# A delta-rule recurrence's DRAM round trip on GpSimd's DMA queue, its merge begun ten steps later, and the latent scan's output products grouped by shape

## The chip, the cores and the metric

The kernel runs on one core of one Trainium2 chip, in one launch. The time is device microseconds (us) of an execution, and the median of several is compared. The engines are named as in the profile: PE is TensorE's matmul stream, PEld its weight loads, DVE VectorE, ACT ScalarE, POOL GpSimd, and SP SyncE, whose queue (SPq) issues nearly all DMAs.

## The reference

Two blocks in a row, all in float32, on 256 positions of 1024 channels. The first has two layers: a norm, an input projection, windowed attention and a pooling mixer, an output projection, and a feed-forward part with 4096 channels. The second has one layer and three branches (a gated delta rule, a short convolution, a Fourier mix), a gated merge and a SwiGLU. The change touches the delta rule alone, which runs in both directions, first over a context of 256 positions and from its end state over the latent positions:

```python
a = jnp.where(strict, jnp.einsum("bhnid,bhnjd->bhnij", kb, k) * decay, 0.0)
t_inv = lax.linalg.triangular_solve(a + eye, eye, left_side=True, lower=True, unit_diagonal=True)
...
def step(s, inp):
    u_i, w_i, qg_i, kd_i, attn_i, gl_i = inp
    v_new = u_i - jnp.einsum("bhcd,bhde->bhce", w_i, s)
    o_i = jnp.einsum("bhcd,bhde->bhce", qg_i, s) + jnp.einsum("bhij,bhje->bhie", attn_i, v_new)
    s = s * jnp.exp(gl_i)[..., None, None] + jnp.einsum("bhcd,bhce->bhde", kd_i, v_new)
    return s, o_i
```

There are 4 chunks of 64 positions, 4 heads of 128 channels and 2 directions, so 32 lower triangular matrices of 64 x 64 are inverted for the context and 32 for the latent positions. Only the latent scan gives outputs.

## The kernel before

**Weights.** Nearly all of PE's time goes into products with weights, which stream through the core once. A weight tile is 128 x 1024. SP loads it into `wst` (`weights`, L256; three buffers, 512 KB each); ACT rounds it to `wh` (L262); DVE subtracts to get the rest, `wl` (L263), each in two halves of 512. `mm3` then makes three products per piece (`wh` with the two halves of the activations, `wl` with the first), all issued at L272. A tile gives 24 matmuls of 256 columns. A load waits for a free `wst`, so for the `wl` of three tiles before; `wl` waits for `wh`, and `wh` for the load.

**Side work.** The second block's modulation and delta rule run beside these products as a generator. `tick` is called once per weight tile and advances it by a rate: 1.2 steps a tile for the context (beside the first block's last feed-forward part), 0.8 for the latent recurrence (beside the short convolution's and the gates' products, woven with the modulation's `w_mod` sums, `wmst`, on DVE). A `yield` ends a step; a scheduler then sets each engine's order, and `issue_after(i)` places an instruction behind `i` on its engine.

**The inverse.** `dn_base` inverts the 16 x 16 diagonal blocks of the triangles on POOL. POOL folds them from `dA` into `ac`; four DMAs write `ac` to DRAM (`there`, L1265, 64 partitions each, in pieces of 16 numbers), one reads them back with a block per partition (`bl`, L1269). Two copies make `blt` (ACT L1273 and DVE L1274, the second transposed). POOL then does fifteen rounds of a product `bo` (L1282) and a subtraction `bz` (L1283), and a transposed copy `bzt` (L1287). Four DMAs write the result to DRAM (`back`, L1291) and four fetch it in the old layout (`xc`, L1299, again in pieces of 16 numbers). The waits between are yields: three after each of the four DMA legs (`wait_dma`), and five among the rounds, 17 in all. `dn_merge` starts with eight multiplications on DVE (`Tm` and `U` from `xc`, L1314), and builds the 64 x 64 inverses from there with PE. There are two such trips, for the context and for the latent positions.

**The scan.** `dn_scan` takes four steps, in each of which both directions handle a chunk. For the eight pairs of head and direction of a latent step it issues two products into the same output tile: the state with the decayed query (`S,qg`; 128 rows of contraction, 64 columns of weights) and the new values with the attention (`dv,att`; 64 and 64), one pair after the other. A product of float32 stands in the trace as two matmul records.

Of the kernel before, what the change touches and what calls it, by code (L numbers as in the profile page):

```python
# [9 lines left out]
F32 = mybir.dt.float32  # L10
F32R = mybir.dt.float32r
I32 = mybir.dt.int32
AF = mybir.ActivationFunctionType
OP = mybir.AluOpType
AX = mybir.AxisListType

P = 128
# [213 lines left out]
class Net:  # L231
# [18 lines left out]
    def weights(self, src, cut=1):  # L250

        nc = self.nc
        st = self.wst.tile([P, 1024], F32, name="wst")
        for c in range(cut):
            cs = slice(c * 1024 // cut, (c + 1) * 1024 // cut)
            nc.sync.dma_start(st[:, cs], src[:, cs])  # L256
        wh = self.wsp.tile([P, 1024], F32R, name="wh")
        wl = self.wsp.tile([P, 1024], F32R, name="wl")
        n = 1024 // self.cutw
        for c in range(0, 1024, n):  # L260
            with self.behind():
                nc.scalar.activation(wh[:, c:c + n], st[:, c:c + n], AF.Copy)  # L262
            (nc.gpsimd if self.onpool > 0 else nc.vector).tensor_tensor(wl[:, c:c + n], st[:, c:c + n], wh[:, c:c + n].bitcast(F32), op=OP.subtract)  # L263
        self.onpool -= 1
        return wh, wl

# [381 lines left out]
    def drain(self):  # L648
        if self.side is not None:
            self.busy = True  # L650
            run(self.side)
            self.busy = False
        self.side = None
# [594 lines left out]
    def dn_base(self, A, X):  # L1248


        nc, pool = self.nc, self.nc.gpsimd
        m = self.k["d_blk"][:, None].to_broadcast([P, 4, 4, 16])
        ac = self.b2.tile([P, 2, 2, 4, 16], F32, name="ac", bufs=1)
        for t in range(2):
            for a in range(2):
                w = self.b2.tile([P, 4, 4, 16], F32, name="bw", tag="gm", bufs=2)
                pool.tensor_tensor(w, A[t][:, a].rearrange("p h (b j) -> p h b j", b=4), m, op=OP.mult)
                pool.tensor_tensor(w[:, :, 0:2], w[:, :, 0:2], w[:, :, 2:4], op=OP.add)
                pool.tensor_tensor(ac[:, a, t], w[:, :, 0], w[:, :, 1], op=OP.add)
            yield  # L1260
        there = self.dram.tile([2, 8, P, 16], F32, name="there")
        for hb in range(2):
            for a in range(2):
                s = slice(64 * hb, 64 * hb + 64)
                nc.sync.dma_start(there[a ^ hb].rearrange("n p j -> p n j")[s], ac[s, a].rearrange("p t h j -> p (t h) j"))  # L1265
        for _ in range(self.wait_dma):
            yield
        L = self.b2.tile([P, 16, 16], F32, name="bl", bufs=1)
        nc.sync.dma_start(L, there.rearrange("d n (q i) j -> (d n q) i j", i=16))  # L1269
        for _ in range(self.wait_dma):  # L1270
            yield
        lt = self.b2.tile([P, 16, 16], F32, name="blt", bufs=1)
        nc.scalar.activation(lt[0:64], L[0:64], AF.Copy)  # L1273
        nc.vector.tensor_copy(lt[64:P], L[64:P].rearrange("p i j -> p j i"))  # L1274
        Z = self.b2.tile([P, 16, 16], F32, name="bz", bufs=1)
        pool.memset(Z, 0.0)
        pool.memset(Z.rearrange("p i j -> p (i j)")[:, 0:256:17], 1.0)
        for j in range(15):
            n, c = 15 - j, j + 1
            o = self.b2.tile([P, 8, 16], F32, name="bo", bufs=1).rearrange("p i j -> p (i j)")[:, 0:n * c]  # L1280
            o = o.rearrange("p (i j) -> p i j", j=c)
            pool.tensor_tensor(o, lt[:, c:, j:c].to_broadcast([P, n, c]), Z[:, j:c, 0:c].to_broadcast([P, n, c]), op=OP.mult)  # L1282
            pool.tensor_tensor(Z[:, c:, 0:c], Z[:, c:, 0:c], o, op=OP.subtract)  # L1283
            if j % 3 == 2:
                yield
        zt = self.b2.tile([P, 16, 16], F32, name="bzt", bufs=1)
        (pool if self.ztp else nc.vector).tensor_copy(zt, Z.rearrange("p i j -> p j i"))  # L1287
        back = self.dram.tile([2, 2, 8, P, 16], F32, name="back")
        for dr in range(2):
            for x in range(2):  # L1290
                nc.sync.dma_start(back[dr, x].rearrange("n (q i) j -> (n q) (i j)", i=16),  # L1291
                               (Z, zt)[x ^ dr][64 * dr:64 * dr + 64].rearrange("p i j -> p (i j)"))
        for _ in range(self.wait_dma):
            yield
        xc = self.b2.tile([P, 2, 2, 2, 4, 16], F32, name="xc", bufs=1)
        for hb in range(2):
            for a in range(2):
                s = slice(64 * hb, 64 * hb + 64)
                nc.sync.dma_start(xc[s, a].rearrange("p x t h j -> p (x t h) j"),  # L1299
                               back[a ^ hb].rearrange("x n p j -> p (x n) j")[s])  # L1300
        for _ in range(self.wait_dma):
            yield
        X["X"] = xc

    def dn_merge(self, d, t, e, A, xc):

        nc, k = self.nc, self.k
        full = [P, 2, 4, CHUNK]
        Tm = self.b2.tile(full, F32, name="Tm")
        U = self.b2.tile(full, F32, name="U")  # L1310
        m = k["d_blk"][:, None].to_broadcast([P, 4, 4, 16])
        for x, o in enumerate((Tm, U)):
            for a in range(2):
                nc.vector.tensor_mul(o[:, a].rearrange("p h (b j) -> p h b j", b=4),  # L1314
                                     xc[:, a, x, t][:, :, None, :].to_broadcast([P, 4, 4, 16]), m)
        for n in range(2):
            al = self.b2.tile(full, F32, name="al")
            nc.vector.tensor_mul(al, A, k["d_lev"][:, :, n][:, :, None, :].to_broadcast(full))
            yb = self.bank().rearrange("p (a h j) -> p a h j", a=2, h=4)
            for a, h, hb, s in self.halves():  # L1320
                self.mm(yb[s, a, h], al[s, a, h], U[s, a, h])
            y = self.b2.tile(full, F32, name="dy")
            nc.scalar.activation(y.rearrange("p a h j -> p (a h j)"), yb.rearrange("p a h j -> p (a h j)"), AF.Copy)
            yield
            ub = self.bank().rearrange("p (a h j) -> p a h j", a=2, h=4)
            for a, h, hb, s in self.halves():
                self.mm(ub[s, a, h], Tm[s, a, h], y[s, a, h])
            if n == 0:
                yield
                tb = self.bank().rearrange("p (a h j) -> p a h j", a=2, h=4)  # L1330
                for a, h, hb, s in self.halves():
                    self.mm(tb[s, a, h], y[s, a, h], Tm[s, a, h])
            nc.vector.tensor_sub(U, U, ub)
            if n == 0:
                nc.vector.tensor_sub(Tm, Tm, tb)
            yield
        W = self.b2.tile(full, F32, name="W")
        nc.vector.tensor_mul(W, U, d["beta"][:, t][:, :, :, None].to_broadcast(full))
        e["W"] = W
# [8 lines left out]
    def dn_scan(self, d, e, S, res):  # L1348
        nc = self.nc
        lat = "q" in d  # L1350
        S = S[-1] if S else None
        if lat:
            ot = [self.dbank().rearrange("p j (q c) -> p (j q) c", c=P) for _ in range(2)]
            res.extend(ot)
        hh = [(h, hb, slice(64 * hb, 64 * hb + 64)) for h in range(4) for hb in range(2)]
        full = [P, 4, P]
        for step, (t, a) in enumerate(STEPS):
            x = e[t]
# [24 lines left out]
            if lat:  # L1383
                v1 = self.sm.tile(full, F32, name="dv1", tag="w2k", bufs=self.nw2k)
                nc.scalar.activation(v1.rearrange("p h c -> p (h c)"), nb.rearrange("p h c -> p (h c)"), AF.Copy)
                q = self.dn_query(d, t, a)
                for h, hb, s in hh:
                    o = ot[t][s, h]
                    self.mm(o, q[:, h, s], S[:, 4 * (a ^ hb) + h], step < 2 and h == 0, False, True)
                    self.mm(o, x["att"][s, a, h], v1[s, h], False, step >= 2, True)  # L1390
            yield
            if last:
                break
# [13 lines left out]
            S = N  # L1407
# [313 lines left out]
    def run(self):  # L1721
# [35 lines left out]
        self.ctx_rate = 1.2  # L1757
        self.scan_rate = 1.8
        self.mod_rate = 0.8
        self.wait_dma = 3  # L1760
        self.mod_parts = (((1, 0, 2), (3,), (4, 5)), ((1, 0, 2), (), (3, 4, 5)), ((1, 0, 2, 3), (), (4, 5)), ((1, 0), (), (2, 3, 4, 5)))[1]
        with ExitStack() as ctx:
            self.ctx = ctx
# [45 lines left out]
```

## Time and profile before

| | |
|---|---|
| median of 3 runs | 1269.43 us (1269.08 to 1270.76) |
| profiled execution | 1270.11 us, span 1268.3 us |
| mean granted clock of PE | 0.975 |
| PE busy | 1202.9 us, 95% of the span |
| DVE, ACT, POOL busy | 900.3, 636.4, 100.1 us |
| DMA | 221.44 MB, mean 175 GB/s |

A share of the whole span says little of one place: the windows split the busy time by stretches, the waits say which instruction an engine waited for, and the timelines give single instructions with the idle time before them and its releaser in brackets. In a row, `out<-in` names tiles, `128*64` is a matmul's rows of contraction and columns of weights, and `xN` is a count. The busy time of POOL is rough.

### The profile page before, as it was taken

How to read it: one execution, taken by the hardware profiler on the slowest of the kernel's cores; microseconds unless marked ns; L12 is line 12 of the kernel's file. 1: busy time of each engine (PE TensorE's matmuls, PEld its weight loads, DVE VectorE, ACT ScalarE, POOL GpSimd, SP SyncE). 2: the span in 40 equal slices, each digit the busy share in tenths (PEclk: the TensorE clock that was granted, in tenths of full speed). 3: DMA queues.
4: the chain of work that ended last, by engine and by line, in shares of the span. 5: the costliest groups of instructions: out<-in, count | busy, mean ns of one | idle time of the engine just before them, and what ended most of it. 6: DMA issues, size and time to landing. Idle time of an engine off the chain costs nothing.

```text
span 1268.3 us, 24741 instructions
## 1 busy us (share of the span) xinstructions
PE 1202.9 (95%) x9858; PEld 1130.2 (89%) x9858; DVE 900.3 (71%) x1786; ACT 636.4 (50%) x1249; POOL 100.1 (8%) x183
## 2 busy tenths in 40 slices
PE   8999999999999989979999799998999997999997
PEld 6779999999977989979999789898888796999997
DVE  6998986557986587636558899987555476555555
ACT  5655445455655555534545656444432354544444
POOL 1000000000100000330000410542000002000000
PEclk9999999999999989989999899998999997999998
DMA  6656787554543535346544415687432252655552
GB/s 231 237 193 217 253 298 255 188 187 149 186 163 127 200 128 186 105 140 202 184 163 139 158 67 188 229 275 234 148 111 74 76 189 85 196 180 190 184 183 83
DMA packets 78388, 221.44 MB, mean 175 GB/s; under 512 B 22336, under 2 KB 24512, under 8 KB 78272
## 3 DMA queue, kind: packets, MB, share of 16 engines
q1 hardware_dynamic: 78272, 219.86, 51.7%
q8 instruction: 77, 1.26, 0.4%
q14 instruction: 39, 0.32, 0.1%
HBM read 218.00 MB, written 1.84 MB: 173 GB/s over the span
## 4 chain that ended last, share of the span: by engine, by line
PE 62%; issue 14%; DVE 12%; DMA 5%; POOL 3%; ACT 2%; SPq 1%; DVEq 0%; ACTq 0%; POOLq 0%
PE acc L272 35%; PE bank L272 26%; DVE wl L263 3%; DMA wmst<-w_mod 2%; POOL bo L1282 1%; POOL bz L1283 1%; ACT wh L262 1%; DVE wmst L880 1%; DVE cy L1034 1%; PE bank L563 1%; DMA wst<-w_in 1%; DVE xl L296 1%; PE bank L368 1%; DVE qkT L531 1%; DMA pt<-pT 0%
## 5 line engine op out<-in xcount | busy, mean ns | idle before, releaser
L262 ACT ACTIVATE wh<-wst 128x512 fp32r<-128x512 f32 x708 | 411.3, 623 | 456.1 <-PE bank L272 148.6
L263 DVE TENSOR_TENSOR wl<-wst,wh 128x512 fp32r<-128x512 f32 x696 | 465.6, 702 | 228.1 <-ACT wh L262 226.2
L272 PE MATMUL bank<-xh,wh 128*128 128x256 f32 x1024 | 295.5, 289 | 9.4 <-ACT wh L262 8.3
L272 PE MATMUL bank<-xl,wh 128*128 128x256 f32 x1024 | 294.2, 287 | 2.0 <-DVE xl L296 2.0
L272 PE MATMUL bank<-xh,wl 128*128 128x256 f32 x1024 | 293.9, 287 | 1.5 <-DVE wl L263 1.5
L272 PEld LDWEIGHTS bank<-xh,wh 128*128 128x128 f32 x1024 | 200.0, 195 | 11.1 <-ACT wh L262 9.1
L272 PEld LDWEIGHTS bank<-xl,wh 128*128 128x128 f32 x1024 | 200.0, 195 | 2.7 <-DVE xl L296 2.6
L272 PEld LDWEIGHTS bank<-xh,wl 128*128 128x128 f32 x1024 | 199.8, 195 | 2.6 <-DVE wl L263 2.5
L272 PE MATMUL acc<-ah,wl 128*128 128x256 f32 x688 | 192.4, 280 | 2.5 <-DVE wl L263 2.5
L272 PE MATMUL acc<-ah,wh 128*128 128x256 f32 x688 | 192.8, 281 | 0.0
L272 PE MATMUL acc<-al,wh 128*128 128x256 f32 x688 | 192.3, 280 | 0.0
L272 PE MATMUL acc<-xh,wl 128*128 128x256 f32 x640 | 184.1, 289 | 5.3 <-DVE wl L263 5.0
L272 PE MATMUL acc<-xh,wh 128*128 128x256 f32 x640 | 185.7, 290 | 0.5 <-ACT wh L262 0.5
L272 PE MATMUL acc<-xl,wh 128*128 128x256 f32 x640 | 183.7, 288 | 0.4 <-DVE xl L910 0.4
L272 PEld LDWEIGHTS acc<-ah,wl 128*128 128x128 f32 x688 | 129.9, 189 | 2.8 <-DVE wl L263 2.7
L272 PEld LDWEIGHTS acc<-xh,wl 128*128 128x128 f32 x640 | 124.2, 194 | 7.4 <-DVE wl L263 6.9
L272 PEld LDWEIGHTS acc<-ah,wh 128*128 128x128 f32 x688 | 129.8, 189 | 0.0
L272 PEld LDWEIGHTS acc<-al,wh 128*128 128x128 f32 x688 | 129.6, 188 | 0.0
L272 PEld LDWEIGHTS acc<-xh,wh 128*128 128x128 f32 x640 | 124.6, 195 | 3.6 <-issue 1.9
L272 PEld LDWEIGHTS acc<-xl,wh 128*128 128x128 f32 x640 | 124.5, 195 | 2.1 <-issue 1.0
L272 PE MATMUL acc<-wl,xh 128*128 128x512 f32 x176 | 69.6, 395 | 3.3 <-DVE wl L263 3.3
L272 PE MATMUL acc<-wh,xh 128*128 128x512 f32 x176 | 69.4, 398 | 1.7 <-ACT wh L262 1.7
(339 smaller groups left out, 1510.6 us busy)
## 6 DMA issues: line engine op xcount, KB each, us to landing
wst<-w_up SPq DMA_DIRECT2D x64, 512.0 KB, 3.7
wst<-w_down SPq DMA_DIRECT2D x64, 512.0 KB, 3.3
wmst<-w_mod SPq DMA_DIRECT2D x48, 512.0 KB, 4.7
wst<-w_fin SPq DMA_DIRECT2D x44, 512.0 KB, 3.2
wst<-w_in SPq DMA_DIRECT2D x39, 512.0 KB, 3.4
wst<-w_mgate SPq DMA_DIRECT2D x24, 512.0 KB, 3.4
wst<-w_fout SPq DMA_DIRECT2D x22, 512.0 KB, 3.2
wst<-w_qkv SPq DMA_DIRECT2D x20, 512.0 KB, 3.3
```

Source lines behind the costliest of these rows:

```text
L262: nc.scalar.activation(wh[:, c:c + n], st[:, c:c + n], AF.Copy)
L263: (nc.gpsimd if self.onpool > 0 else nc.vector).tensor_tensor(wl[:, c:c + n], st[:, c:c + n], wh[:, c:c + n].bitcast(F32), op=OP.subtract)
L272: self.nc.tensor.matmul(out, lhsT, rhs, start=start, stop=stop, skip_group_check=skip)
L296: nc.vector.scalar_tensor_tensor(xl[:, k], src, gain, xh[:, k].bitcast(F32), op0=OP.mult, op1=OP.subtract)
L368: self.nc.tensor.transpose(bk[:, i * P:(i + 1) * P], c[:, i:i + 1].to_broadcast([P, P]), self.ident)
L531: nc.vector.tensor_copy(qk[:, :, t * P:(t + 1) * P], bk.rearrange("p (c q) -> p c q", c=4))
L563: nc.tensor.transpose(bk[:, c * P:(c + 1) * P], s[:, g, c * P:(c + 1) * P], self.ident)
L880: nc.vector.scalar_tensor_tensor(pr, st, 1.0, cv[v], op0=OP.mult, op1=OP.mult, accum_out=mod[:, part, v, k:k + 1])
L1034: nc.vector.scalar_tensor_tensor(y4[:, j], pad[:, j, :, tap:tap + CHUNK], w[:, j, tap:tap + 1], y4[:, j], op0=OP.mult, op1=OP.add)
L1282: pool.tensor_tensor(o, lt[:, c:, j:c].to_broadcast([P, n, c]), Z[:, j:c, 0:c].to_broadcast([P, n, c]), op=OP.mult)
L1283: pool.tensor_tensor(Z[:, c:, 0:c], Z[:, c:, 0:c], o, op=OP.subtract)
```

## The change

All thirteen DMAs of a trip are issued by POOL; both copies to `blt` are POOL's; the yields within the trip are gone and ten stand behind its last DMA. `dn_merge`'s eight multiplications are placed behind the last `wl` that DVE was given before them. In the scan, the eight `S,qg` products of a step come first, then the eight `dv,att`. In the changed kernel the lines after L263 are two higher up to `there` (L1267; `bl` stays at L1269), then lower: `blt` L1271 and L1272, `bo` L1280, `bz` L1281, `bzt` L1283, `back` L1287, `xc` L1293, `Tm` and `U` L1309; the matmuls' L272 is L274.

```diff
@@ weights: the last VectorE split of a weight is remembered
-            (nc.gpsimd if self.onpool > 0 else nc.vector).tensor_tensor(wl[:, c:c + n], ...)
+            i = (nc.gpsimd if self.onpool > 0 else nc.vector).tensor_tensor(wl[:, c:c + n], ...)
+            if self.onpool <= 0:
+                self.lastwl = i.ins
@@ dn_base: the round trip
-                nc.sync.dma_start(there[a ^ hb].rearrange("n p j -> p n j")[s], ac[s, a].rearrange("p t h j -> p (t h) j"))
-        for _ in range(self.wait_dma):
-            yield
+                pool.dma_start(there[a ^ hb].rearrange("n p j -> p n j")[s], ac[s, a].rearrange("p t h j -> p (t h) j"))
         L = self.b2.tile([P, 16, 16], F32, name="bl", bufs=1)
-        nc.sync.dma_start(L, there.rearrange("d n (q i) j -> (d n q) i j", i=16))
-        for _ in range(self.wait_dma):
-            yield
+        pool.dma_start(L, there.rearrange("d n (q i) j -> (d n q) i j", i=16))
         lt = self.b2.tile([P, 16, 16], F32, name="blt", bufs=1)
-        nc.scalar.activation(lt[0:64], L[0:64], AF.Copy)
-        nc.vector.tensor_copy(lt[64:P], L[64:P].rearrange("p i j -> p j i"))
+        pool.tensor_copy(lt[0:64], L[0:64])
+        pool.tensor_copy(lt[64:P], L[64:P].rearrange("p i j -> p j i"))
...
-            if j % 3 == 2:
-                yield
...
-                nc.sync.dma_start(back[dr, x].rearrange("n (q i) j -> (n q) (i j)", i=16),
+                pool.dma_start(back[dr, x].rearrange("n (q i) j -> (n q) (i j)", i=16),
...
-        for _ in range(self.wait_dma):
-            yield
...
-                nc.sync.dma_start(xc[s, a].rearrange("p x t h j -> p (x t h) j"),
+                pool.dma_start(xc[s, a].rearrange("p x t h j -> p (x t h) j"),
...
-        for _ in range(self.wait_dma):
+        for _ in range(self.trip):
             yield
@@ dn_merge: its first eight multiplications
-        for x, o in enumerate((Tm, U)):
-            for a in range(2):
-                nc.vector.tensor_mul(...)
+        with self.tc.issue_after(self.lastwl):
+            for x, o in enumerate((Tm, U)):
+                for a in range(2):
+                    nc.vector.tensor_mul(...)
@@ dn_scan: output products of one step
                 for h, hb, s in hh:
-                    o = ot[t][s, h]
-                    self.mm(o, q[:, h, s], S[:, 4 * (a ^ hb) + h], step < 2 and h == 0, False, True)
-                    self.mm(o, x["att"][s, a, h], v1[s, h], False, step >= 2, True)
+                    self.mm(ot[t][s, h], q[:, h, s], S[:, 4 * (a ^ hb) + h], step < 2 and h == 0, False, True)
+                for h, hb, s in hh:
+                    self.mm(ot[t][s, h], x["att"][s, a, h], v1[s, h], False, step >= 2, True)
@@
-        self.wait_dma = 3
+        self.trip = 10
```

POOL at the context's trip before the change: `ac` is the folded blocks, `bo` and `bz` the rounds; no DMA stands on this queue.

```order
L1259 TENSOR_TENSOR ac<-bw 128x64 x2
L1282 TENSOR_TENSOR bo<-blt,bz 128x15
L1283 TENSOR_TENSOR bz<-bz,bo 128x15
L1282 TENSOR_TENSOR bo<-blt,bz 128x28
```

POOL at the same place with the change, from the last `ac` to the first round:

```order
L1261 TENSOR_TENSOR ac<-bw 128x64 x2
L1267 DMA there<-ac 64x8x16 x4
L1269 DMA bl<-there 128x256
L1271 COPY blt<-bl 64x256
L1272 COPY blt<-bl 64x256
L1280 TENSOR_TENSOR bo<-blt,bz 128x15
L1281 TENSOR_TENSOR bz<-bz,bo 128x15
```

and from the last round to the clearing of the next trip's `bz`:

```order
L1281 TENSOR_TENSOR bz<-bz,bo 128x15
L1283 COPY bzt<-bz 128x256
L1287 DMA back<-bz 64x256
L1287 DMA back<-bzt 64x256 x2
L1287 DMA back<-bz 64x256
L1293 DMA xc<-back 64x16x16 x4
L1274 MEMSET bz 128x256
```

The thirteen DMAs and the two copies now stand between POOL's own instructions. On SP's queue they stood among the weight loads; this is the latent trip's second half there before the change (`w_mgate` and `w_sc_out` are weights, `wmst<-w_mod` the modulation's):

```order
L1291 DMA back<-bz 64x256
L256 DMA wst<-w_mgate 128x1024
L1291 DMA back<-bzt 64x256 x2
L1291 DMA back<-bz 64x256
L876 DMA wmst<-w_mod 128x1024
L256 DMA wst<-w_mgate 128x1024
L256 DMA wst<-w_sc_out 128x1024
L876 DMA wmst<-w_mod 128x1024
L256 DMA wst<-w_mgate 128x1024
L876 DMA wmst<-w_mod 128x1024
L256 DMA wst<-w_mgate 128x1024
L1299 DMA xc<-back 64x16x16
```

With the change, only the rows of `wst` and `wmst` are left of it.

DVE at the start of the latent merge before the change (`wl` is a weight's rest, `wmst,mod` a `w_mod` sum, `h` the gates):

```order
L880 SCALAR_TENSOR_TENSOR wmst,mod<-wmst,cv_1273 128x1024
L263 TENSOR_TENSOR wl<-wst,wh 128x512 x4
L880 SCALAR_TENSOR_TENSOR wmst,mod<-wmst,cv_1273 128x1024
L1500 SCALAR_TENSOR_TENSOR h<-bg,acc 128x256 x2
L263 TENSOR_TENSOR wl<-wst,wh 128x512 x2
L880 SCALAR_TENSOR_TENSOR wmst,mod<-wmst,cv_1273 128x1024
L263 TENSOR_TENSOR wl<-wst,wh 128x512 x2
L884 TENSOR_TENSOR mod<-mod,k_b_mod 128x8
L263 TENSOR_TENSOR wl<-wst,wh 128x512 x2
L1314 TENSOR_TENSOR Tm<-xc,k_d_blk 128x256
L1314 TENSOR_TENSOR U<-xc,k_d_blk 128x256
L1500 SCALAR_TENSOR_TENSOR h<-bg,acc 128x256 x2
```

DVE at the same place with the change:

```order
L1495 SCALAR_TENSOR_TENSOR h<-bg,acc 128x256 x2
L263 TENSOR_TENSOR wl<-wst,wh 128x512 x2
L882 SCALAR_TENSOR_TENSOR wmst,mod<-wmst,cv_1273 128x1024
L263 TENSOR_TENSOR wl<-wst,wh 128x512 x2
L1309 TENSOR_TENSOR Tm<-xc,k_d_blk 128x256 x2
L1309 TENSOR_TENSOR U<-xc,k_d_blk 128x256 x2
L1309 TENSOR_TENSOR Tm<-xc,k_d_blk 128x256 x2
L1309 TENSOR_TENSOR U<-xc,k_d_blk 128x256 x2
L263 TENSOR_TENSOR wl<-wst,wh 128x512 x2
L1495 SCALAR_TENSOR_TENSOR h<-bg,acc 128x256 x2
L263 TENSOR_TENSOR wl<-wst,wh 128x512 x2
```

The eight multiplications stand together, and nearer to the trip: two pairs of `wl` behind the `h` row above, where before there were six (the last five stand in the rows before the change, the `h` row ahead of them is left out). In the context, counted from the last `dA` in the same way, `Tm` stands 15 pairs of `wl` later than before.

PE in the scan before the change, behind the last product of a step's state update:

```order
L272 MATMUL bank<-dv_11418,tokk 128x128 x2
L272 MATMUL acc<-S,qg 64x128
L272 MATMUL acc<-dv_11420,att 64x128
L272 MATMUL acc<-S,qg 64x128
L272 MATMUL acc<-dv_11420,att 64x128
L272 MATMUL acc<-S,qg 64x128
L272 MATMUL acc<-dv_11420,att 64x128
```

With the change, in a step:

```order
L274 MATMUL bank<-dv_11098,tokk 128x128 x3
L274 MATMUL acc<-S,qg 64x128 x8
L274 MATMUL acc<-dv_11100,att 64x128 x8
L274 MATMUL acc<-k_f_pos,fu 128x258 x4
```

The two shapes alternated eight times; now each of them stands in one row.

## Rows read from the trace of the kernel before

**Rows 1.** Windows: us, busy PE, PEld, DVE, ACT, POOL, PEclk, DMA share, GB/s.

```profile
540.00:560.00 20.00, 17.31 (x131) 16.89 (x131) 9.32 (x16) 7.00 (x13) 9.65 (x23) 0.91 0.43 133
560.00:580.00 20.00, 12.56 (x81) 11.93 (x81) 8.34 (x17) 6.90 (x12) 2.82 (x12) 0.86 0.60 165
```

**Rows 2.** Waits of PE and SP's queue, 535 to 590: us, times, longest.

```profile
PE bank L272 <- ACT wh L262: 7.4, 2, 5.0
PE acc L272 <- DVE wl L263: 2.5, 1, 2.5
...
SPq L1291 <- POOL bz L1283: 11.8, 1, 11.8
```

**Rows 3.** Timeline of SP's queue, context trip: start, us, instruction.

```profile
562.25 0.48 SPq L1291 DMA_DIRECT2D back<-bz  x1
```

**Rows 4.** DMA share in tenths, 40 slices of 536 to 575.

```profile
DMA  0058999972098005920000000000398896979999
```

**Rows 5.** Windows at half clock and at full, columns as in rows 1.

```profile
567.50:570.80 3.30, 3.30 (x14) 3.07 (x15) 2.67 (x5) 2.70 (x5) 0.33 (x4) 0.50 0.90 186
590.00:593.30 3.30, 3.30 (x30) 3.30 (x29) 2.29 (x5) 2.31 (x4) 0.00 (x0) 1.00 0.47 164
872.90:878.00 5.10, 5.09 (x24) 5.09 (x25) 4.86 (x9) 2.58 (x7) 0.00 (x0) 0.50 0.79 286
```

**Rows 6.** Timeline of VectorE and PE behind the latent trip.

```profile
863.59 1.54 DVE L263 TENSOR_TENSOR wl<-wst,wh 128x512 fp32r<-128x512 f32 x2
...
871.02 1.22 DVE L880 SCALAR_TENSOR_TENSOR wmst<-wmst,cv 128x1024 f32<-128x1024 f32 x1 [4.80 <-DMA wmst<-w_mod]
...
868.58 0.39 PE L272 MATMUL acc<-xh,wh 128*128 128x256 f32 x1 [0.49 <-ACT wh L262]
...
872.91 0.58 PE L272 MATMUL acc<-xh,wl 128*128 128x256 f32 x1 [3.83 <-DVE wl L263]
```

**Rows 7.** Windows of one step's output products and of two runs of one shape.

```profile
946.67:952.45 5.78, 5.78 (x34) 3.03 (x33) 1.29 (x2) 1.62 (x4) 0.00 (x0) 1.00 0.28 91
940.56:941.59 1.03, 1.03 (x17) 0.85 (x16) 0.37 (x1) 1.03 (x2) 0.00 (x0) 1.00 0.34 64
944.06:945.07 1.01, 1.01 (x17) 0.85 (x16) 0.00 (x0) 0.00 (x0) 0.00 (x0) 1.00 0.96 260
```

**Rows 8.** Timeline of VectorE: the first multiplication of the context's merge.

```profile
573.72 0.43 DVE L1314 TENSOR_TENSOR Tm<-xc,k_d_blk 128x256 f32<-128x256 f32 x1 [2.40 <-DMA xc<-back]
```

**Rows 9.** Timeline of POOL in the context trip.

```profile
535.95 1.50 POOL L1259 TENSOR_TENSOR ac<-bw 128x64 f32<-128x64 f32 x2
...
548.59 0.22 POOL L1282 TENSOR_TENSOR bo<-blt,bz 128x15 f32<-128x15 f32 x1 [11.14 <-ACT blt L1273]
...
562.29 0.60 POOL L1287 COPY bzt<-bz 128x256 f32<-128x256 f32 x1
```

**Rows 10.** DMA issues of 820 to 885: count, KB each, median us to landing.

```profile
xc<-back SPq DMA_DIRECT2D x4, 64.0 KB, 5.0
there<-ac SPq DMA_DIRECT2D x4, 32.0 KB, 2.2
bl<-there SPq DMA_DIRECT2D x1, 128.0 KB, 4.6
...
back<-bzt SPq DMA_DIRECT2D x2, 64.0 KB, 3.4
```

**Rows 11.** The trip's DMAs by tile: ns of one issue, min/median/max.

```profile
L1269 SPq DMA_DIRECT2D bl<-there x2: 326/332/337, 545.7 to 829.1; - x2
...
L1299 SPq DMA_DIRECT2D xc<-back x8: 573/624/2345, 566.9 to 880.1; - x8
```

**Rows 12.** Timeline of POOL in the latent trip.

```profile
824.81 0.32 POOL L1259 TENSOR_TENSOR ac<-bw 128x64 f32<-128x64 f32 x1
...
842.48 0.74 POOL L1282 TENSOR_TENSOR bo<-blt,bz 128x15 f32<-128x15 f32 x1 [17.26 <-ACT wh L262]
...
863.35 0.63 POOL L1287 COPY bzt<-bz 128x256 f32<-128x256 f32 x1
```

More of the change, by code (lines that the diff above doesn't have):

```diff
@@ L262, in weights @@
                 nc.scalar.activation(wh[:, c:c + n], st[:, c:c + n], AF.Copy)
-            (nc.gpsimd if self.onpool > 0 else nc.vector).tensor_tensor(wl[:, c:c + n], st[:, c:c + n], wh[:, c:c + n].bitcast(F32), op=OP.subtract)
+            i = (nc.gpsimd if self.onpool > 0 else nc.vector).tensor_tensor(wl[:, c:c + n], st[:, c:c + n], wh[:, c:c + n].bitcast(F32), op=OP.subtract)
+            if self.onpool <= 0:
+                self.lastwl = i.ins
         self.onpool -= 1
@@ L1311, in dn_merge @@
         m = k["d_blk"][:, None].to_broadcast([P, 4, 4, 16])
-        for x, o in enumerate((Tm, U)):
-            for a in range(2):
-                nc.vector.tensor_mul(o[:, a].rearrange("p h (b j) -> p h b j", b=4),
-                                     xc[:, a, x, t][:, :, None, :].to_broadcast([P, 4, 4, 16]), m)
+        with self.tc.issue_after(self.lastwl):
+            for x, o in enumerate((Tm, U)):
+                for a in range(2):
+                    nc.vector.tensor_mul(o[:, a].rearrange("p h (b j) -> p h b j", b=4),
+                                         xc[:, a, x, t][:, :, None, :].to_broadcast([P, 4, 4, 16]), m)
         for n in range(2):
```

## The prediction

> **What bounds the kernel now.** I read the busy table first: TensorE (PE) works 95% of the span, so time can only be won where PE stands idle, runs below its pace, or works longer than its data need. The windows of 20 us show one such place [rows 1]: in 540 to 580 us PE is busy 17.31 and 12.56 of two times 20 us, so 10.1 us are idle, and its granted clock falls to 0.91 and 0.86.
>
> The waits of that stretch name the releasers [rows 2]: ScalarE's first half of a weight (`wh`), 7.4 us, and VectorE's second half (`wl`), 2.5 us. Both come late because the load ahead of them is late. The queue of SyncE (SP) shows why: it waited 11.8 us in one piece for GpSimd's (POOL's) last `bz` [rows 2], and issued `back` at 562.25 [rows 3]. The weight loads stand behind that transfer. The DMA line of the stretch, 40 slices of just under 1 us [rows 4], has ten in a row at 0, so the DMA engines were idle too: the queue was blocked, not the memory.
>
> After each of these stalls PE runs at half its clock for 3.4 us, three times. One of the three [rows 5]: 14 matmuls in 3.30 us at clock 0.50 (1.2 GHz), against 30 at clock 1.00 (2.4 GHz) in as much time. Each costs half of 3.4, 1.7 us, together 5.1.
>
> The latent trip has a smaller loss [rows 6]: VectorE waits 4.80 us for a `w_mod` load that stood behind the trip's DMAs, PE then 3.83 us for `wl`, and 24 matmuls take 5.10 us at clock 0.50 [rows 5], for which 24/30 of 3.30, 2.64, would do: 2.5 us more. With PE's 0.49 us of wait just ahead [rows 6] that is 6.8 us, of which 4.3 are idle.
>
> Last, the output products of the latent scan [rows 7]. One step's 32 matmul records take 5.78 us with PE busy throughout, in each of the four steps. The same shapes in a run of their own go much faster: 16 of 128*64 in 1.03 us (`S,kT`), 16 of 64*64 in 1.01 us (`dr,W`).
>
> **Grouping by shape.** Sixteen `S,qg` now stand together, then sixteen `dv,att`. At the pace of these two runs a step takes 1.03 + 1.01 = 2.04 us instead of 5.78, 3.74 us less, and four steps 15.0. I take 14.8, since two changes of shape per step stay. PE is the limit there, so this comes off the end. The ends of this term are 0, if the slow pace belongs to accumulating two products into one tile, and 15.0. Nearest are the rows of like shapes, hence 14.8.
>
> **The context trip.** Four `there`, one `bl`, four `back` and four `xc`, 13 DMAs in all, leave SP's queue, and 17 waiting yields become 10 behind the last transfer. SP then holds weight loads only, so PE's 10.1 us of idle and 5.1 us of half pace go: 15.2. The cover is VectorE's work before it reaches `Tm`. Before, `Tm` began at 573.72 after 2.40 us for `xc` [rows 8], so VectorE was there at 571.3, already late by 7.6 us of PE idle (the 10.1 less the 2.5 of [rows 2], which came after it) and by two stretches of half pace, 3.4: 560 undisturbed. In the order of the change, `Tm` stands 15 weight tiles later; with 24 matmuls at full pace [rows 5], 2.64 us a tile, that is 600.
>
> The trip on POOL: let X be what one DMA costs on POOL's queue. `ac` ends at 537.45 [rows 9]; landings 2.2 (`there`), 4.6 (`bl`), 3.4 (`back`), 5.0 (`xc`), those of the busier latent trip [rows 10]; two copies and two clears about 1.6, by POOL's own copy of 0.60 [rows 9]; the fifteen rounds and `bzt` from 548.59 to 562.89, 14.3 [rows 9]. Landings count from the start of an issue, so some 2 us lie in both. The end is 567 + 13X, under 600 while X is below 2.6. The new wait on VectorE costs nothing up to there; behind it are the next `wl`, and PE behind those.
>
> **X** is in no row: POOL issued no DMA. SP's rows of the same transfers [rows 11] are the bounds: 0.33 at the least (`bl`), 0.62 as the median of `xc`, 2.345 at the most. I take 0.9: SP's 0.62 times 21.5/14.3, by which POOL's rounds of the latent trip, 842.48 to 863.98 [rows 12], are longer than the context's, VectorE being busy beside them.
>
> **The latent trip.** Here the cover is thin. POOL's `ac` ends at 825.1 [rows 12]; with the same landings, copies 1.6 and rounds 21.5 the trip ends at 825.1 + 2.2 + 4.6 + 1.6 + 21.5 + 3.4 + 5.0 - 2 + 13X = 861 + 13X. With X = 0.9 that is 873. In the new order `Tm` comes one `w_mod` sum (1.22) and one more pair of `wl` (1.54) after the pair that ended at 865.13 before [rows 6]: VectorE is there at about 868, and stands. PE then still has the tile of that last pair, the one it began at 868.58 before [rows 6], and is out of work 2.64 us later, near 871.2. Behind the end of the trip stand eight multiplications (0.43 each [rows 8], overlapping, some 3.0) and half a pair of `wl`, 0.7. PE idles 861 + 13X + 3.7 - 871.2 = 13X - 6.5: 5.2 us, and 2.5 of half pace after it as before. So 6.8 is won and 7.7 lost: **+0.9**. The ends: nothing idle at X = 0.5 or less, -6.8; at 2.345, 24.0 + 2.5 - 6.8 = +19.7.
>
> Two copies (0.4 us each) leave ScalarE and VectorE, which don't bind there. Fewer yields bring later steps to other tiles; scan and merge fill waits as before, and in the scan no wait of PE shows [rows 7], so I price them at zero. Were that cover gone, a step would cost its own chain, a few us, inside the range.
>
> **Sum.** -14.8 - 15.2 + 0.9 = -29.1 against the profiled execution, 1270.11 us: 1241.0. That execution lies 0.7 over the median of the runs shown, 1269.43, so I predict **1240**.
>
> **Rivals.**
> - *B, the latent trip is covered.* X at SP's shortest price or rounds as short as in the context. Then -14.8 - 15.2 - 6.8 = -36.8: **1233**. For: 13X - 6.5 is zero at 0.5, and POOL's rounds alone could give 7 us. Against: POOL's rounds, on POOL alone, did take the 21.5 [rows 12], so its issues there will hardly be cheap.
> - *C, POOL's issues are held up by VectorE.* POOL's latent rounds took 21.5 us where the context's took 14.3 [rows 9, 12], so something there halves its speed. If each issue also waits for one `wl` in flight (1.54 us for two [rows 6]), X is 0.9 + 0.7 = 1.6, the latent term +10.0 (14.3 idle and 2.5 of clock less 6.8) and the time **1249**; with SP's longest price, 1259. The Trainium skill, SBUF — State Buffer, section Who interferes with whom, has a rule for this: a DMA issued from GpSimd has its descriptors written by GpSimd's cores, and a VectorE instruction that holds the shared port keeps them from writing. No run here shows a DMA from POOL.
> - *D, grouping pays nothing.* The slow pace belongs to the accumulation: 1270.1 - 15.2 + 0.9 - 0.7 = **1255**. Against: the plain runs of both shapes [rows 7].
> - *F, moving the issues does not do what it says*, since the transfers meet on the same DMA engines whichever queue starts them; only grouping pays, **1255**. Against: idle DMA engines while SP waited [rows 4]. The Trainium skill, DMA: Bandwidth & Descriptors, section Issuing engines are not separate DMA queues, says that starting DMAs on several engines saves only the sequencer's time to start them, usually small beside the transfer. By this the sum would be -14.8; the trace disagrees, as SP's sequencer was held 11.8 us.
> - *E, slower.* A price per piece: `xc` moves 64.0 KB [rows 10] in pieces of 16 numbers, 64 bytes, 1024 in each of four transfers; were each piece written out by POOL, X would be several us. From X = 2.6 on the context's cover is gone too. There the latent term is +23.0, the sum -7.0; from then on both trips add 13 each per us, and 2.5 of clock. It crosses zero near X = 2.8. At X = 4 it is -7.0 + 2.5 + 36.4 = +32: **1301**. Place: VectorE at `Tm`, waiting for `xc`. For: nothing in the trace excludes it. Against: SP's own highest price for these same pieces, 2.345 [rows 11].
>
> **How the numbers follow.** Forecast 0.48, B 0.21, C 0.15, D 0.05, F 0.03, E 0.08. A measurement of this kernel tells about 0.2% (2.5 us) from no change; E holds 0.02 inside that and 0.06 beyond it, everything else is faster: 0.92, 0.02, 0.06. The range runs from 1231, a little under B, to 1257, over C, D and F but short of C's far end; outside lie E (0.08), the top of C (0.03) and 0.05 under 1231.
>
> **What would show it.** Right: SP without a wait on `bz`; PE without waits between 535 and 600 and its clock at full there; `S,qg` and `dv,att` together near 8 us of span over four steps, not 23; VectorE at the latent `Tm` with about 5 us of wait on `xc`, and PE idle about as long behind it. POOL's DMA rows give X, and so separate B, C and E. Wrong: idle PE near the context's `Tm`, products at the old pace, or SP queue waits that stay.

## The result, and the profile after

The changed kernel takes 1238.17 us (median of 4 runs, 1237.42 to 1240.33) against 1269.26 for the kernel before in the same comparison: a ratio of 0.9759, 95% interval 0.9741 to 0.9777. The profiled execution took 1240.33 us.

The page of the changed kernel, busy us with share and instructions of each engine:

```profile
PE 1183.0 (96%) x9858; PEld 1122.1 (91%) x9858; DVE 899.4 (73%) x1784; ACT 636.3 (51%) x1247; POOL 124.7 (10%) x213
```

PE does the same 9858 instructions in 19.9 us less of busy time than before (1202.9): that is the products at their new pace, and less work at half clock. The windows of the context trip [rows 1], and of one scan step [rows 7], have changed places with full ones (columns as there):

```profile
540.00:560.00 20.00, 20.00 (x170) 20.00 (x170) 12.19 (x22) 10.38 (x18) 11.00 (x24) 1.00 0.64 207
560.00:580.00 20.00, 20.00 (x170) 20.00 (x169) 12.18 (x22) 10.38 (x18) 10.55 (x25) 1.00 0.78 211
...
903.23:905.35 2.12, 2.12 (x34) 1.77 (x33) 0.75 (x2) 2.03 (x5) 0.00 (x0) 1.00 0.00 0
```

In the context PE has no idle time and full clock. Between 530 and 620 us, the waits of SP's queue are these two; the wait on `bz` [rows 2] is gone:

```profile
SPq L256 <- DVE wl L263: 77.0, 30, 6.7
SPq L256 <- DMA wst<-w_up: 0.2, 1, 0.2
```

To see which part gave what, I take a point that both traces have: the first matmul behind a norm, where PE waits for VectorE's `rsy`. It comes once between the context trip and the latent trip, and once after the scan. Here it is before the change (timeline of PE):

```profile
725.09 0.45 PE L368 MATMUL bank<-k_c_ident,rsy 128*128 128x128 f32 x1 [6.61 <-DVE rsy L359]
...
1063.54 0.47 PE L368 MATMUL bank<-k_c_ident,rsy 128*128 128x128 f32 x1 [7.47 <-DVE rsy L359]
```

and in the changed kernel:

```profile
710.46 0.45 PE L370 MATMUL bank<-k_c_ident,rsy 128*128 128x128 f32 x1 [6.59 <-DVE rsy L361]
...
1033.50 0.69 PE L370 MATMUL bank<-k_c_ident,rsy 128*128 128x128 f32 x2 [7.59 <-DVE rsy L361]
```

At the first point the changed kernel is 14.6 us ahead: the context trip. At the second it is 30.0 ahead, 15.4 more. Four steps at 5.78 - 2.12 = 3.66 us make 14.6 of these, so 0.8 is left for the latent trip and all else between the two points. At the end the spans differ by 29.8.

The latent trip has kept a stall of its own. Timeline of VectorE and PE in the changed kernel, the context's first multiplication, then the latent's and the PE instruction behind it:

```profile
600.68 0.42 DVE L1309 TENSOR_TENSOR Tm<-xc,k_d_blk 128x256 f32<-128x256 f32 x1
...
860.79 0.76 DVE L1309 TENSOR_TENSOR Tm<-xc,k_d_blk 128x256 f32<-128x256 f32 x2 [8.24 <-DMA xc<-back]
...
861.94 1.33 PE L274 MATMUL bank<-U,al 64*64 64x64 f32 x20 [6.72 <-DVE U L1309]
```

In the context no wait is named at `Tm`; in the latent part VectorE stands 8.24 us for `xc` and PE 6.72 us for the merge.

### The profile page after: what moved, and what is told of

Same layout as the page of the kernel before. It is cut to its first block, busy times and chain, and to the rows that moved or that the text cites. A ratio compares the mean times of both kernels' runs of the same rounds, so it can differ in the third digit from the quotient of the medians.

```text
span 1238.5 us, 24745 instructions
## 1 busy us (share of the span) xinstructions
PE 1183.0 (96%) x9858; PEld 1122.1 (91%) x9858; DVE 899.4 (73%) x1784; ACT 636.3 (51%) x1247; POOL 124.7 (10%) x213
## 3 DMA queue, kind: packets, MB, share of 16 engines
q0 software_dynamic: 864, 1.57, 0.7%
## 4 chain that ended last, share of the span: by engine, by line
PE 64%; issue 13%; DVE 12%; POOL 6%; DMA 4%; ACT 1%; DVEq 0%; SPq 0%; POOLq 0%; ACTq 0%
PE acc L274 34%; PE bank L274 28%; DVE wl L263 3%; POOL bo L1280 1%; POOL bz L1281 1%; DVE cy L1036 1%; PE bank L565 1%; DVE xl L298 1%; DVE wmst L882 1%; DMA bl<-there 1%; DMA xc<-back 1%; ACT wh L262 1%; POOL bw L1259 1%; DMA wmst<-w_mod 1%; DVE qkT L533 1%
## 5 line engine op out<-in xcount | busy, mean ns | idle before, releaser
L263 DVE TENSOR_TENSOR wl<-wst,wh 128x512 fp32r<-128x512 f32 x696 | 464.9, 700 | 216.7 <-ACT wh L262 216.0
L274 PE MATMUL bank<-xh,wh 128*128 128x256 f32 x1024 | 293.9, 287 | 2.0 <-ACT xh L911 1.1
L274 PE MATMUL bank<-xl,wh 128*128 128x256 f32 x1024 | 293.0, 286 | 1.8 <-DVE xl L298 1.8
L274 PE MATMUL bank<-xh,wl 128*128 128x256 f32 x1024 | 292.6, 286 | 1.6 <-DVE wl L263 1.6
L274 PEld LDWEIGHTS bank<-xh,wh 128*128 128x128 f32 x1024 | 198.6, 194 | 3.2 <-ACT xh L911 1.5
L274 PEld LDWEIGHTS bank<-xh,wl 128*128 128x128 f32 x1024 | 198.6, 194 | 2.8 <-DVE wl L263 2.6
L274 PEld LDWEIGHTS bank<-xl,wh 128*128 128x128 f32 x1024 | 198.6, 194 | 2.5 <-DVE xl L298 2.4
L274 PE MATMUL acc<-ah,wh 128*128 128x256 f32 x688 | 192.1, 280 | 0.0
L274 PE MATMUL acc<-al,wh 128*128 128x256 f32 x688 | 191.7, 279 | 0.0
L274 PE MATMUL acc<-ah,wl 128*128 128x256 f32 x688 | 191.6, 279 | 0.0
L274 PE MATMUL acc<-xh,wh 128*128 128x256 f32 x640 | 184.5, 289 | 0.4 <-ACT wh L262 0.4
L274 PE MATMUL acc<-xl,wh 128*128 128x256 f32 x640 | 183.2, 287 | 0.4 <-DVE xl L912 0.4
L274 PE MATMUL acc<-xh,wl 128*128 128x256 f32 x640 | 182.8, 286 | 0.5 <-DVE wl L263 0.4
L274 PEld LDWEIGHTS acc<-ah,wl 128*128 128x128 f32 x688 | 129.2, 188 | 0.1
L274 PEld LDWEIGHTS acc<-ah,wh 128*128 128x128 f32 x688 | 129.1, 188 | 0.0
L274 PEld LDWEIGHTS acc<-al,wh 128*128 128x128 f32 x688 | 128.9, 187 | 0.0
L274 PEld LDWEIGHTS acc<-xh,wh 128*128 128x128 f32 x640 | 124.0, 194 | 2.8 <-issue 1.4
L274 PEld LDWEIGHTS acc<-xl,wh 128*128 128x128 f32 x640 | 123.9, 194 | 2.1 <-issue 1.0
L274 PEld LDWEIGHTS acc<-xh,wl 128*128 128x128 f32 x640 | 123.8, 194 | 1.3 <-DVE wl L263 0.9
L274 PE MATMUL acc<-wl,xh 128*128 128x512 f32 x176 | 70.6, 401 | 2.3 <-DVE wl L263 2.3
L274 PE MATMUL acc<-wh,xh 128*128 128x512 f32 x176 | 70.6, 405 | 1.5 <-ACT wh L262 1.5
```

Of the source, the lines that this page charges most:

```text
L263: i = (nc.gpsimd if self.onpool > 0 else nc.vector).tensor_tensor(wl[:, c:c + n], st[:, c:c + n], wh[:, c:c + n].bitcast(F32), op=OP.subtract)
L274: self.nc.tensor.matmul(out, lhsT, rhs, start=start, stop=stop, skip_group_check=skip)
```

## The experiments

**Each part alone.** First the kernel before with the products grouped:

```diff
-                    o = ot[t][s, h]
-                    self.mm(o, q[:, h, s], S[:, 4 * (a ^ hb) + h], ...)
-                    self.mm(o, x["att"][s, a, h], v1[s, h], ...)
+                    self.mm(ot[t][s, h], q[:, h, s], S[:, 4 * (a ^ hb) + h], ...)
+                for h, hb, s in hh:
+                    self.mm(ot[t][s, h], x["att"][s, a, h], v1[s, h], ...)
```

> The kernel before with the scan's output products grouped by shape and nothing else. Theory (every change of shape costs PE time, and PE is the limit there): -14.9 us against before, about 1254.4; S,qg and dv,att some 2.2 us a step instead of 5.8, the context's stalls as before. Rival (the gain belongs to the trip, or the scan waits for something else once its products are short): under 5 us of gain.

Measured: 1256.24 us, ratio 0.9889 (0.9862 to 0.9917), which is 14.1 us of 1268.67; the medians differ by 12.4. The groups of the two products in its trace (busy us and mean ns of one):

```profile
L272 PE MATMUL acc<-S,qg 128*64 128x128 f32 x64 | 4.4, 279 | 0.0
L272 PE MATMUL acc<-dv,att 64*64 64x128 f32 x64 | 4.4, 275 | 0.0
```

The theory holds. Then the changed kernel with the same lines put back:

> The changed kernel with the scan's products alternating again. Theory: the trip's part is worth 14.6 us in the context and nearly nothing in the latent part, so about 1253 us, 14.9 over the changed kernel. Rival (the two parts overlap, the earlier end of one eats the other): the two parts alone do not add up to the whole 31 us, off by more than 4.

Measured: 1251.46 us, 0.9861 (0.9840 to 0.9881), 17.6 us, by the medians 17.2. The two add up to 31.7 by the ratios and to 29.6 by the medians; the whole is 31.1. No overlap shows, though with intervals of 3.5 and 2.6 us to either side the times alone could hide one of about 4. The traces show the parts apart: with grouping alone PE still waits 6.9 us for `wh` in the context (7.4 in [rows 2]), and with the trip alone it waits for nothing between 535 and 600 us while the scan's products keep their old pace. So the rival falls. That the trip alone looks 2 us better than at the two points of PE above is within that interval.

**Queue or late merge?** The changed kernel, with the DMAs on SP's queue again and all else left:

```diff
-                pool.dma_start(...)
+                nc.sync.dma_start(...)
```

at all four legs.

> The changed kernel with the trip's thirteen DMAs on SyncE's queue again; the copies stay on GpSimd and the merge stays late. Theory (the weight loads stand behind the trip's DMAs on one queue): SyncE waits about 12 us for the rounds again, PE idles 8 to 12 us in the context with half clock behind it, about 1250 us. Rival (it is the later merge alone that brings the gain; or a queue's place does not matter since all meet on the same DMA engines): within 2 us of the changed kernel, 1238.

Measured: 1258.79 us, ratio 0.9920 (0.9899 to 0.9940): 20.6 us over the changed kernel, somewhat more than expected. Its waits, 530 to 880 us (us, times, longest), on SP's queue and PE:

```profile
SPq L1287 <- POOL bz L1281: 29.3, 2, 15.0
...
PE acc L274 <- ACT wh L262: 13.4, 3, 10.0
PE bank L274 <- ACT wh L262: 11.1, 1, 11.1
```

SP waits for the rounds in both trips, and PE for the weights behind it, 11.1 us in the context and 10.0 in the latent part. The late merge by itself does not help: with grouping alone the time was 1256.24. Without yields among the legs the queue blocks for longer than before, 14.3 us in the context against 11.8 [rows 2]. The rule that issuing engines are not separate DMA queues (the Trainium skill, DMA: Bandwidth & Descriptors, section Issuing engines are not separate DMA queues) would leave this within a little issue time of the changed kernel. The trace disagrees: what a queue costs here is its waiting, 29.3 us, not its issuing.

The same on ScalarE's queue (`nc.scalar.dma_start`):

> The changed kernel with the trip's DMAs on ScalarE's queue. Theory (a queue that waits for the rounds holds up whatever stands behind it; GpSimd has nothing behind it): ScalarE's halves of the weights wait for the rounds, PE idles about 10 us in each trip, about 1258 us, as on SyncE's queue. Rival (SyncE is the wrong queue only because of the weight loads; the loads have three buffers, the halves too, and ScalarE is idle half the time): within 3 us of 1238.

Measured: 1256.53 us, 0.9911 (0.9891 to 0.9931). PE's two longest waits between 530 and 880 us:

```profile
PE acc L274 <- ACT wh L262: 11.5, 1, 11.5
PE bank L274 <- ACT wh L262: 9.0, 1, 9.0
```

About 10 us a trip, as the theory says. ScalarE's spare time does not help: its instructions come in order, and those behind a waiting DMA wait too. In the context its next `wh`, behind the four `back`, began at 557.25 after 13.35 us of idle ScalarE. GpSimd is the right queue since next to nothing that PE needs stands behind the trip there.

**The anchor or the ten steps?** The changed kernel without the ordering edge:

```diff
-        with self.tc.issue_after(self.lastwl):
+        with ExitStack():
```

> The changed kernel without the line that places the merge's eight multiplications behind the last weight split; the ten steps stay. In the order the context's multiplications then stand 18 weight tiles earlier and the first of the latent's 7 earlier. Theory (the anchor, not the ten steps, is the cover): VectorE waits for xc some 25 us in the context and some 25 in the latent part, PE behind it, about 1280 us. Rival (the ten steps are the cover, the scheduler's place is harmless): within 3 us of 1238.

Measured: 1264.12 us, 0.9966 (0.9949 to 0.9983), 26 us over the changed kernel and not the 42 expected. VectorE's first wait, 530 to 880 us:

```profile
DVE Tm L1309 <- DMA xc<-back: 37.0, 2, 20.4
```

20.4 and 16.6 us; PE is idle behind them for 16.0 and 15.1. So the anchor is the cover: ten steps alone let the scheduler put the multiplications as far up as their tile is free. I overrated the size because the trip ended earlier, too. While VectorE stands, POOL's rounds go faster: 11.1 us in the context, where it stood throughout them, against 15.2 in the changed kernel (windows in the last section). Of the latent ones VectorE stood beside the second half, from 844.86 on (timeline of POOL, first and last row):

```profile
836.58 1.08 POOL L1280 TENSOR_TENSOR bo<-blt,bz 128x15 f32<-128x15 f32 x1
...
852.25 0.60 POOL L1283 COPY bzt<-bz 128x256 f32<-128x256 f32 x1
```

That is 16.3 us, where the changed kernel needs 23.8 (its rows stand further down).

**Shape or accumulation?** The changed kernel with four `S,qg`, then `dv,att` and `S,qg` by turns, so that no `dv,att` stands right behind the `S,qg` of its own tile:

```diff
-                for h, hb, s in hh:
-                    self.mm(ot[t][s, h], q[:, h, s], S[...], ...)
-                for h, hb, s in hh:
-                    self.mm(ot[t][s, h], x["att"][s, a, h], v1[s, h], ...)
+                one = lambda h, hb, s: self.mm(ot[t][s, h], q[:, h, s], S[...], ...)
+                two = lambda h, hb, s: self.mm(ot[t][s, h], x["att"][s, a, h], v1[s, h], ...)
+                for i in range(12):
+                    if i >= 4:
+                        two(*hh[i - 4])
+                    if i < 8:
+                        one(*hh[i])
```

> The changed kernel with the step's products in another order: four S,qg, then dv,att and S,qg by turns, then four dv,att, so that the shape changes nine times in a step (sixteen times with its two ends before the change, once or twice with it) while no two products in a row go into the same output tile. Theory (the change of shape costs, some 0.25 us each): eight changes more per step, 2.1 us, 8.5 in four steps, about 1247 us; a step near 4.1 us. Rival (the cost was two products in a row that add into one output tile): as the changed kernel, 1238, a step near 2.1 us.

Measured: 1245.10 us, 0.9811 (0.9792 to 0.9830), 6.9 us over the changed kernel. Its first step in the timeline of PE:

```profile
900.88 0.66 PE L274 MATMUL acc<-S,qg 128*64 128x128 f32 x8
901.47 0.43 PE L274 MATMUL acc<-dv,att 64*64 64x128 f32 x2
901.83 0.43 PE L274 MATMUL acc<-S,qg 128*64 128x128 f32 x2
...
904.36 0.65 PE L274 MATMUL acc<-dv,att 64*64 64x128 f32 x8
```

and its window:

```profile
900.87:905.02 4.15, 4.15 (x34) 2.42 (x33) 1.38 (x2) 2.04 (x5) 0.00 (x0) 1.00 0.11 28
```

No two products in a row share a tile here, and a step still takes 4.15 us. Within a step the shape changes nine times here, once in the changed kernel and fifteen times before. Eight changes of shape cost 4.15 - 2.12 = 2.03, so 0.25 us each; the fourteen that the change removes cost 5.78 - 2.12 = 3.66, 0.26 each. The same price both times: it is the shape. The Trainium skill, TensorEngine Tiling (Array Packing), section Key Properties, says that a change of tiling mode drains TensorE; this trace agrees so far as each change costs time, and gives the price.

**What is left of the latent trip.** More steps behind it, for the latent part alone:

```diff
+            self.trip = 13
             yield from self.dn_prep(dl, el)
```

> The changed kernel with thirteen steps behind the latent trip instead of ten; the context keeps ten. The multiplications then stand five weight tiles, some 14 us, later. Theory (what is left of the latent trip is VectorE standing 8.2 us at Tm for xc): the wait and PE's 6.7 us of idle go, with about 1.6 of half pace: 1230 us. Rival (the recurrence has no slack behind it: the scan comes later, and its chain or the branches' end then waits): 1236 us or more, with a new wait of PE after 870 us.

Measured: 1237.69 us, 0.9767 (0.9737 to 0.9796): no change that can be told (four executions, 1235.15 to 1243.42). The wait at `Tm` is gone, but PE's waits between 880 and 1010 us, none in the changed kernel, are now

```profile
PE bank L274 <- DVE dr L1367: 4.4, 2, 2.3
PE bank L274 <- DVE dv L1377: 0.4, 2, 0.2
```

The rival holds, by its number. The timeline of PE shows the place:

```profile
901.63 0.28 PE L274 MATMUL acc<-xh,wl 128*128 128x256 f32 x1
901.84 1.09 PE L274 MATMUL bank<-S,kT 128*64 128x128 f32 x16
905.09 1.09 PE L274 MATMUL bank<-dr,W 64*64 64x128 f32 x16 [2.15 <-DVE dr L1367]
```

A scan step's `dr,W` stands right behind its `S,kT`, with no weight products between, so VectorE's work from one to the other is bare. With sixteen steps:

> The same with sixteen steps, eight weight tiles later than with ten. Theory: the cover is already full with thirteen, so the same time within 1 us, 1230. Rival (no slack behind the recurrence): some 5 us or more over thirteen steps.

Measured: 1241.14 us, 0.9778 (0.9759 to 0.9797), 3.5 us over thirteen steps by the medians. The two ratios' intervals overlap, so the times tell neither the theory's 1 us nor the rival's 5. The trace has the waits of thirteen steps again, longer (PE, 880 to 1010 us):

```profile
PE bank L274 <- DVE dr L1367: 5.8, 2, 2.9
```

The order of instructions has `S,kT` and `dr,W` without weights between in two steps with thirteen, and in two with sixteen; in none with ten or with twelve. That gave a sharper theory, in which not lateness counts but the weight tile on which a step falls:

```diff
+            self.trip = 12
             yield from self.dn_prep(dl, el)
```

> The changed kernel with twelve steps behind the latent trip. In the order Tm then stands three weight tiles (8.5 us) later than with ten steps, which is just the 8.2 us that VectorE waited, and no scan step has its products S,kT and dr,W side by side without weight products between them, as two steps had with thirteen. Theory (thirteen steps won the 8 us at Tm and gave them back because two scan steps fell on one weight tile): the 8 us stay won, about 1231 us, no wait of PE on dr after 890 us. Rival (a later merge costs its chain whatever the tiles): about 1237 as with thirteen.

Measured: **1230.59 us**, 0.9712 (0.9691 to 0.9733), 7.6 us under the changed kernel by the medians, 6.0 by the ratios, and faster than both. Of PE's waits between 800 and 1030 us none is left on `U` or `dr`; the two longest the changed kernel has too (7.6 and 1.1):

```profile
PE bank L370 <- DVE rsy L361: 7.7, 1, 7.7
PE bank L274 <- ACT xh L911: 1.1, 1, 1.1
```

The theory holds: what thirteen steps gave back stands in the two waits on `dr`, and twelve steps have neither. A kernel with more than thirteen steps and no such place was not run, so that lateness itself costs nothing is argued from the waits, not shown.

## Why the prediction was right

Forecast 1240, measured 1238.2. The mechanisms of the two large terms held; that the sum lies within 2 us is partly luck, since the errors of the latent trip cancel. The terms, one by one:

**Grouping, -14.8.** 14.6 by the windows; alone 14.1 by the ratio and 12.4 by the medians. Rival D falls by the offset products.

**The context trip, -15.2.** 14.6 at the first checkpoint. VectorE came to `Tm` at 600.68, where 600 was worked out. The trip ended well before: POOL sent its last two `xc` from 571.05 on, 0.81 us each (next fence), which with the median landing of 5.8 us there is about 578. The cover was some 23 us, and X could have been over 2.

**X, 0.9.** Timeline of POOL in the changed kernel, context and then latent:

```profile
538.36 2.90 POOL L1267 DMA_DIRECT2D there<-ac  x4
545.42 0.59 POOL L1269 DMA_DIRECT2D bl<-there  x1 [4.16 <-DMA there<-ac]
...
565.55 0.58 POOL L1287 DMA_DIRECT2D back<-bz  x1
...
571.05 1.62 POOL L1293 DMA_DIRECT2D xc<-back  x2 [0.72 <-DMA back<-bz]
...
821.23 1.07 POOL L1280 TENSOR_TENSOR bo<-blt,bz 128x15 f32<-128x15 f32 x1
...
843.42 1.58 POOL L1283 COPY bzt<-bz 128x256 f32<-128x256 f32 x1
...
851.02 3.28 POOL L1293 DMA_DIRECT2D xc<-back  x4 [3.95 <-DMA back<-bzt]
```

0.72 for `there`, 0.59 for `bl`, 0.52 to 0.58 for `back`, 0.82 for `xc`: 0.69 in the mean. My step from POOL's slower rounds to slower issues failed: `xc` cost 0.82 in both trips. With it rival C falls as an account of the issue, and E altogether.

**The latent trip, +0.9.** By its own rows it came out near +1.5: PE idle for 6.72 us, and 3.22 us of work at half clock behind that, which cost about half, 1.6, less the 6.8 won. The window of that half clock:

```profile
861.94:865.16 3.22, 3.22 (x60) 3.22 (x62) 3.22 (x9) 0.60 (x1) 0.00 (x0) 0.50 0.00 0
```

The remainder between the two points of PE above, -0.8, is 2.3 us lower. That difference lies in PE's work outside this stall and outside the four steps, and no run here shows its cause. That the trip's end decides was right, the sizes of its parts were off in both directions. X was 2.7 us too dear in all. The rounds with `bzt`, 821.23 to 845.00, took 23.8, not 21.5. The landings of `back` and `xc` were longer, as the DMA issues of 808 to 875 us show (count, KB each, median us to landing), against 3.4 and 5.0 in [rows 10]:

```profile
xc<-back POOLq DMA_DIRECT2D x4, 64.0 KB, 7.2
...
back<-bzt POOLq DMA_DIRECT2D x2, 64.0 KB, 4.8
```

What I had wrong is what PE waits for. I let it run dry of weights and start again behind eight multiplications and half a `wl`, 3.7 us after `xc`. In fact it stood at the merge's first product, `bank<-U,al`, which has its place ahead of the next weight, and went on 1.2 us after VectorE started (861.94 less 860.79). The next weight was only half there. ScalarE had made its second `wh` by 853.99, but its `wl` came behind the eight multiplications, as I had it, and PE's first product with it after the merge's (ScalarE, VectorE and PE):

```profile
853.36 0.63 ACT L262 ACTIVATE wh<-wst 128x512 fp32r<-128x512 f32 x1
...
863.48 1.28 DVE L263 TENSOR_TENSOR wl<-wst,wh 128x512 fp32r<-128x512 f32 x2
...
865.40 0.39 PE L274 MATMUL acc<-xh,wh 128*128 128x256 f32 x1
```

So the merge's products gave PE 3.5 us of work while `wl` was made. VectorE waited 8.24 us at `Tm` instead of 5, and PE idled 6.72 us instead of 5.2, but it started again sooner after `xc`.

**Rivals.** B, the covered latent trip at 1233, was not this kernel; it is nearly the twelve-step version, 1230.6. F falls by the trip on SP's queue.

Why did POOL's transfers land later in the latent trip? VectorE's work beside them is not needed for it: from the first issue of `xc` to the last landing VectorE was busy for 1.53 of 9.74 us, in the changed kernel's window

```profile
851.02:860.76 9.74, 4.20 (x36) 4.00 (x34) 1.53 (x4) 3.19 (x7) 3.28 (x4) 0.88 0.71 178
```

and `xc` took its 7.2 us. Without the anchor, where VectorE and the loads both stood, the same issues landed in

```profile
xc<-back POOLq DMA_DIRECT2D x4, 64.0 KB, 3.1
```

That points to the loads on the same DMA engines. Why it was 7.2 us here and 5.8 in the context is not shown.

## What to carry to other kernels

A DMA that has to wait belongs on a queue with nothing urgent behind it, and its price is the work that stands behind the wait, not its issue; a row of zeros in the DMA line beside a waiting queue is the sign. Moving the wait to the reader is only a gain if the reader's place in its engine's order is pinned behind enough work; check that place in the order, then move it by single steps, because a chain that follows can fall on tiles without cover. And on TensorE, put small products of one shape together when each turn from one shape to another shows as a fixed cost.

## What the runs showed of the hardware beyond that

POOL's DMAs come out in far fewer packets. The DMA queues before the change (packets, MB, share):

```profile
q1 hardware_dynamic: 78272, 219.86, 51.7%
```

and after:

```profile
q1 hardware_dynamic: 64800, 218.29, 53.3%
q0 software_dynamic: 864, 1.57, 0.7%
```

1.57 MB took 13472 packets from SP's queue and takes 864 from POOL's. I had feared a price per 64-byte piece; for `xc`, 0.82 us against SP's median of 0.62 [rows 11] is all that shows of it.

The Trainium skill, SBUF — State Buffer, section Who interferes with whom, lets a VectorE instruction hold up the descriptors of a GpSimd DMA, but it found this for `tensor_copy` and not for `tensor_tensor`. The `wl` beside the trips are `tensor_tensor`, and in POOL's issue rows nothing of a hold-up shows, as the section has it for them: `xc` cost 0.82 to 0.85 us an issue with twelve steps, where VectorE was busy for 96% of the latent issues (846.36 to 849.65), and 0.81 to 0.85 without the anchor, where VectorE stood in all of them. POOL's rounds, which are no DMAs, do slow down the more VectorE works beside them. These are the windows from the first `bo` to the end of `bzt` (columns as in rows 1, VectorE's busy time the third behind the length): the context without the anchor, then the context and the latent trip of the changed kernel.

```profile
549.95:561.07 11.12, 5.51 (x47) 5.30 (x45) 0.00 (x0) 1.79 (x4) 8.78 (x32) 0.84 0.11 41
...
550.46:565.62 15.16, 15.16 (x129) 15.16 (x129) 9.46 (x16) 7.78 (x15) 12.82 (x32) 1.00 0.56 189
821.23:845.00 23.77, 23.44 (x196) 23.24 (x195) 23.29 (x40) 11.40 (x22) 21.43 (x32) 1.00 0.86 294
```

So the same rounds took 11.1 us with VectorE idle, 15.2 with it busy for 62% and 23.8 with it busy for 98%.
